# Prompt attention with every matrix product over 128 rows and 128 columns of TensorE

## The chip, the cores and the metric

One core of a Trainium2 chip runs the whole program. The metric is device time in microseconds. Five engines work beside each other, each in its own order: TensorE (PE; its weight loads are shown as PEld), VectorE (DVE), ScalarE (ACT), GpSimd (POOL) and SyncE (SP, which issues most transfers).

## What is computed

The program is one step of a decoder with two layers, for 1024 prompt tokens and 8 sampled tokens (each with 8192 past tokens in a paged cache). Each layer is

```
h = rms_norm(x) ; proj = h @ w_in                # inputs of four groups and a gate z
groups: NSA attention | HGRN2 recurrence | pooling | memory cross-attention
x = x + (silu(z) * concat(groups)) @ w_out
```

The change lies in two of the groups, and there in the prompt's tokens alone. NSA attention has 4 query heads of width 64 over one key-value head, and three branches whose results are gated and added:

```
s_c = q @ kcc.T ; p_c = masked_softmax(s_c)      # 32 compressed blocks of the prompt
s_s = q @ ks.T  ; p_s = masked_softmax(s_s)      # selected blocks (for this length: all causal keys)
s_w = q @ kw.T  ; p_w = masked_softmax(s_w)      # causal window of 512 keys
o = g0 * (p_c @ vcc) + g1 * (p_s @ vs) + g2 * (p_w @ vw)
```

Memory cross-attention has 4 heads of width 64 over 256 memory rows, without a mask. Everything is float32. TensorE multiplies in fp32r, in which an operand is split into a high part and a low rest (hi + lo), so that a product of two operands takes two or three passes.

## The kernel before

Each layer has four phases: A (norm and token-major projections), P2 (prompt attention, memory attention, pooling, and the rest of the projections as filler), P3 (compression of the sampled tokens' cache, recurrence, window) and O (output projection, selected branch of the sampled tokens). The change touches P2.

In P2, `nsa_prompt` goes through 8 tiles of 128 tokens. `nsa_prep` builds for a tile the queries `QS` (partitions 0 to 63 hold one half of hi and lo, 64 to 127 the other, so that one product over 128 rows gives (q_hi + q_lo) · k_hi with the keys' high part `KD` standing twice), the keys' low part `KL` (twice as well), the values `VS` as [hi | lo] in 128 columns, and the compressed branch's probabilities `Pc`, 32 columns a head. `nsa_unit` then works on two of the four heads: for each head and branch the scores' product (line 764), the causal mask as a product of a bf16 identity with a bf16 mask (lines 766 and 768), and the low keys' product, which takes only the 64 rows with the queries' high part (line 769):

```
mm(S, QS[half, h], KL[half, br, ks], start=False, stop=True)
```

VectorE takes the maximum (772), ScalarE the exponential (447), VectorE or GpSimd scales the probabilities (799, 797). They are then transposed in pieces of 128 keys, two pieces for both heads into one bank (`tr`, line 246), cast to hi on ScalarE (819), the rest lo on VectorE (820), and multiplied with the values: hi with 128 columns [hi | lo] (825, 828), lo with the 64 columns of the high values only (826). The compressed piece is the first of the list, with 32 rows, so its pair is cast in two parts. `fold` adds the two column halves of the result.

`mem_unit` does the same for the memory: lines 1150 and 1151 give the scores (the latter over 64 rows), 1168, 1170 and 1171 the values (1170 with 64 columns). The generator `others` runs its units and the pooling group between the units of `nsa_unit`.

The order of instructions on each engine is the planner's: it simulates a time line from its own costs and the priorities given with `prio`. The filler is `stageA2`, three products (lines 120 to 122) of 344 columns for each of 8 chunks, tied with `issue_after` to shares of the attention's own TensorE instructions, so that it is spread between them. PSUM banks of P2: two for scores, three for transposes, one accumulator, and two for the filler.

Of the kernel before, what the change touches and what calls it, by code (L numbers as in the profile page):

```python
# [9 lines left out]
F32 = mybir.dt.float32  # L10
# [80 lines left out]
class Lane:  # L91
    """PSUM tiles of one stream of work: s scores, t transposes, a accumulators, as (columns, buffers); own: tags with a pool for each bank"""
# [20 lines left out]
class Net:  # L113
# [14 lines left out]
    def cc(self, pool, name):  # L128
        """a constant that only one stage uses"""
# [22 lines left out]
    def rsqrt(self, y, x, pool, tag="rs"):  # L152
        """y = x ** -0.5 for [p, n] views"""
# [11 lines left out]
    # ---------------------------------------------------------------- setup  # L165
    def setup(self, ctx):
# [5 lines left out]
        self.identb = self.cp.tile([128, 128], BF, name="identb")  # L172
        self.mdiag = self.cp.tile([128, 128], BF, name="mdiagb")
        self.mfar = self.cp.tile([128, 128], BF, name="mfarb")
# [20 lines left out]
        self.zero = self.cp.tile([128, 320], F32, name="zero")  # L195
# [3 lines left out]
    def late_setup(self, tp):  # L199
        """constants that the first stage does without"""  # L200
        nc, a = self.nc, self.a
        nc.vector.tensor_copy(self.identb, self.ident)
# [5 lines left out]
        # numbers of the row pairs of every other four pages, among all row pairs of the cache  # L208
# [39 lines left out]
    # ---------------------------------------------------------------- stage A: norm and projections  # L248
# [23 lines left out]
    def alloc_hT(self, l, hp):  # L272
# [4 lines left out]
        nc.vector.tensor_copy(self.hS.rearrange("p k c -> p (k c)"), self.zero)  # L277
# [22 lines left out]
    def tokmajor(self, w, n, i, pieces, out, xp, lo_out=False):  # L300
        """out [p, n] = rows of token tile i times w; pieces: stationary views per k, sampled tokens as [hi | lo]"""
# [23 lines left out]
    def stageA1(self, l, wp, xp):  # L325
        """token-major projections: NSA queries, keys, values and gates, HGRN values, memory queries"""
# [34 lines left out]
    def stageA2(self, l, mts, wp, xp, **kw):  # L361
        """feature-major projections, one block of 128 features at a time"""
# [21 lines left out]
    def headnorm(self, x, gain, pool, tag):  # L384
        """x [p, h, 64] normalised over 64 in place; gain [p, 64] or [p, h, 64]"""
# [84 lines left out]
    def cpe(self, l, wp):  # L470
        """position rows with the halves of the feature axis as the weights have them"""
# [21 lines left out]
    def cweights(self, l, cp):  # L493
        """first layer's weights, a piece [128, 8, 256] for each half of the positions; w[t][c] = (hi, lo)"""
# [16 lines left out]
    def cload(self, l, u, g, xp, rb):  # L511
        """raw rows of 8 pages: two tokens to a partition; gives the pairs of [k0 k1] and of [v1 v0]; no u: the prompt's rows"""
# [62 lines left out]
    def csilu(self, hid, n, bB, xp):  # L575
        """2 silu of the hidden rows, feature-major, split"""
# [20 lines left out]
    def cout(self, hh, hl, n, W):  # L597
# [5 lines left out]
        # the values' two products with the weights' halves lie side by side  # L603
# [20 lines left out]
    def cprompt(self, l, wp, xp, other):  # L624
        """the 32 blocks of the prompt, in float32 products: the weights pass once"""
# [5 lines left out]
        for t in range(2):  # L631
# [20 lines left out]
            # what the position rows give alone is the bias of the sampled tokens' blocks  # L652
# [5 lines left out]
        # for the heads of either half: [hi | lo of that half's rows]  # L658
        nc.vector.tensor_copy(self.Kc.rearrange("p e s n -> p (e s n)"), self.zero[:, :128])
# [8 lines left out]
        nc.scalar.copy(self.VcP[:, 0:64], vc)  # L668
        nc.vector.tensor_tensor(self.VcP[:, 64:128], vc, self.VcP[:, 0:64].bitcast(F32), op=OP.subtract)

    # ---------------------------------------------------------------- stage B: mixing
    def oput(self, c, col, n, o):
        """spill a piece of the mixed features (feature-major) until the output projection"""
        self.nc.sync.dma_start(self.od[c][:, col:col + n], o)

    def nsa_prompt(self, l, pp, wk, other):
        """one step of the other stream after each pair of heads"""
# [3 lines left out]
        mcmp = self.cc(pp, "mcmp")  # L681
        nxt = self.nsa_prep(0, KV, mcmp, wk)
# [11 lines left out]
    def nsa_prep(self, i, KV, mcmp, wk):  # L694
        """queries [hi; lo] of token tile i, its keys and values, probabilities of the compressed branch"""
# [25 lines left out]
        # compressed branch  # L721
        Pc = wk.tile([128, 4, 32], F32, name="Pcmp")
# [13 lines left out]
        # rows without a complete block have no such branch  # L736
# [4 lines left out]
        return QS, Pc  # L741

    def nsa_unit(self, i, hp, QS, KV, Pc, wk, oT):
# [11 lines left out]
        for e in range(2):  # L755
            h = 2 * hp + e
            half = slice(e * 64, e * 64 + 64)
            for br in range(2):
                n = nw if br else nk
                c1 = n if C == 1 else (384 if br else 512)  # L760
                for c, (c0, m) in enumerate(((0, c1), (c1, n - c1))[:C]):
# [21 lines left out]
        else:  # L783
            # bring the chunks to their common maximum
# [10 lines left out]
        for p, w in chunks:  # L795
# [4 lines left out]
        jobs = [(None, 32, self.VcP)] + [(1024 + 128 * j, 128, VS[:, w0 // 128 + j, 1]) for j in range(nw // 128)] \  # L800
            + [(128 * j, 128, VS[:, j, 0]) for j in range(i + 1)]
        O = self.psA()
        last = len(jobs) - 1
        for g in range(0, len(jobs), 2):
            pair = jobs[g:g + 2]
            ps = self.psT()
            kmax = max(k for _, k, _ in pair)
            for j, (c0, k, _) in enumerate(pair):
                for e in range(2):
                    src = Pc[:, 2 * hp + e] if c0 is None else Pt[:, e, c0:c0 + k]  # L810
                    self.tr(ps[:k, j * 256 + e * 128:j * 256 + e * 128 + 128], src)
            ph = wk.tile([128, 512], F32R, name="ph", bufs=2)
            pl = wk.tile([128, 512], F32R, name="pl", bufs=2)
            if all(k == kmax for _, k, _ in pair):
                sp = [(kmax, 0, 256 * len(pair))]
            else:
                sp = [(k, 256 * j, 256 * j + 256) for j, (_, k, _) in enumerate(pair)]
# [987 lines left out]
```

## Time and profile before

| | |
|---|---|
| time, median of 3 runs | 2352.56 us (2349.35 to 2356.87) |
| span of the profiled execution | 2347.0 us |
| PE busy | 2133.6 us, 91% (14396 products) |
| PEld busy | 1831.8 us, 78% |
| DVE busy | 1535.0 us, 65% |
| ACT busy | 892.9 us, 38% |
| POOL busy | 751.9 us, 32% |

The time of the profiled execution itself is not listed; its span runs from its first to its last instruction, and the median of the timed runs lies 5.6 us above it. Busy times are sums over the span, and engines overlap. A product's duration in a row contains its way through the array, which overlaps the next product; the distance from one start to the next is what the stream of products pays.

### The profile page before, as it was taken

The numbers are of one execution on the slowest core, as the hardware profiler recorded it, in microseconds if no ns is written. First come the engines' busy times: TensorE is split into PE (matmuls) and PEld (weight loads), VectorE is DVE, ScalarE is ACT, GpSimd is POOL, SyncE is SP. The second block draws the span as 40 slices with busy tenths as digits, with TensorE's granted clock in tenths as the row PEclk, the third lists the DMA queues.
The fourth block names the chain that finished last, engine by engine and source line by source line (L and its number), as shares of the span: only waits on it lengthen the run. The fifth ranks groups of instructions, "written<-read, shape, count | busy, mean of one in ns | idle before, by whom it ended". The sixth has DMA issues, their size and how long they took to land.

```text
span 2347.0 us, 42103 instructions
## 1 busy us (share of the span) xinstructions
PE 2133.6 (91%) x14396; PEld 1831.8 (78%) x14396; DVE 1535.0 (65%) x4069; ACT 892.9 (38%) x2145; POOL 751.9 (32%) x837
## 2 busy tenths in 40 slices
PE   4999999999699999889969999999986899999898
PEld 4997887777588888777669978777776788887775
DVE  7874355797687776575288723678876777765643
ACT  4223355655443333331152234555546333322311
POOL 2002111422465554342220011233134556642430
PEclk8999997999699999989989999989987999999899
DMA  6236321211865455867453362211147455557672
GB/s 240 96 113 185 89 61 36 68 40 59 220 174 141 131 143 129 234 197 218 152 171 105 112 154 82 73 47 52 34 108 206 134 140 147 143 158 226 187 221 106
DMA packets 324094, 312.98 MB, mean 133 GB/s; under 512 B 60619, under 2 KB 285783, under 8 KB 323608
## 3 DMA queue, kind: packets, MB, share of 16 engines
q1 hardware_dynamic: 261544, 213.25, 31.2%
q0 software_dynamic: 24320, 79.71, 11.7%
q10 hardware_dynamic: 38016, 17.32, 2.8%
q8 instruction: 115, 1.88, 0.3%
q14 instruction: 99, 0.81, 0.1%
HBM read 255.00 MB, written 59.57 MB: 134 GB/s over the span
## 4 chain that ended last, share of the span: by engine, by line
PE 58%; DVE 13%; DMA 12%; issue 7%; POOL 5%; ACT 3%; SPq 1%; ACTq 0%; DVEq 0%; POOLq 0%
PE mt L246 4%; DMA R<-in_cache_nsa_dram 3%; PE aa L122 3%; PE aa L121 3%; DMA R<-in_cache_nsa_dram,idxc 3%; PE aa L120 3%; PE oa L122 2%; PE oa L120 2%; PE oa L121 2%; PE ch L122 2%; PE ch L120 2%; PE ms L769 2%; PE ch L121 2%; PE ct L246 2%; PE fa L120 2%
## 5 line engine op out<-in xcount | busy, mean ns | idle before, releaser
L524 POOL DMA_INDIRECT R<-in_cache_nsa_dram,idxc x256 | 253.0, 988 | 226.8 <-PE ct L246 138.6
L120 PE MATMUL ch<-w1h,Xh 128*128 128x256 f32 x1024 | 310.6, 303 | 10.3 <-ACT Xh L564 9.2
L122 PE MATMUL ch<-w1h,Xl 128*128 128x256 f32 x1024 | 309.4, 302 | 7.7 <-DVE Xl L565 7.5
L121 PE MATMUL ch<-w1l,Xh 128*128 128x256 f32 x1024 | 306.6, 299 | 0.0
L120 PEld LDWEIGHTS ch<-w1h,Xh 128*128 128x128 f32 x1024 | 207.3, 202 | 14.8 <-ACT Xh L564 10.9
L122 PEld LDWEIGHTS ch<-w1h,Xl 128*128 128x128 f32 x1024 | 207.4, 203 | 14.0 <-DVE Xl L565 10.5
L148 POOL TENSOR_TENSOR wl<-wf,wh 128x1024 fp32r<-128x1024 f32 (+2 forms) x42 | 92.7, 2217 | 374.7 <-ACT wh L139 293.6
L121 PEld LDWEIGHTS ch<-w1l,Xh 128*128 128x128 f32 x1024 | 207.3, 202 | 3.4 <-issue 2.1
L564 ACT CAST Xh<-ct 128x512 fp32r<-128x512 f32 x256 | 145.6, 585 | 146.5 <-PE ct L246 100.9
L246 PE MATMUL ct<-cst,R 128*128 128x128 f32 x1024 | 161.3, 287 | 37.6 <-DVE Xl L565 32.7
L565 DVE TENSOR_TENSOR Xl<-ct,Xh 128x512 fp32r<-128x512 f32 x256 | 171.1, 681 | 25.8 <-ACT Xh L564 25.0
L544 DVE COPY R<-R 128x256 f32<-128x256 f32 x260 | 95.1, 383 | 117.2 <-DMA R<-in_cache_nsa_dram,idxc 100.4
L120 PE MATMUL aa<-wh,hTh 128*128 128x326 f32 (+1 forms) x512 | 156.6, 307 | 5.2 <-ACT wh L139 5.2
L121 PE MATMUL aa<-wl,hTh 128*128 128x326 f32 (+1 forms) x512 | 156.4, 306 | 3.8 <-POOL wl L148 3.8
L246 PEld LDWEIGHTS ct<-cst,R 128*128 128x128 f32 x1024 | 118.5, 146 | 48.6 <-DVE Xl L565 33.3
L122 PE MATMUL aa<-wh,hTl 128*128 128x326 f32 (+1 forms) x512 | 155.9, 305 | 0.0
L772 DVE TENSOR_REDUCE nst<-ms 128x1 f32<-128x512 f32 (+3 forms) x192 | 99.0, 520 | 69.3 <-PE ms L769 66.8
L120 PE MATMUL fa<-hTh,wh 128*128 128x344 f32 x384 | 132.7, 346 | 2.5 <-ACT fo L381 2.5
L819 ACT CAST ph<-mt 128x512 fp32r<-128x512 f32 (+2 forms) x192 | 90.6, 484 | 100.9 <-PE ma L825 47.5
L447 ACT ACTIVATE P<-ms,nst 128x512 f32<-128x512 f32 (+3 forms) x192 | 106.1, 554 | 58.9 <-DVE nst L772 56.9
L121 PE MATMUL fa<-hTl,wh 128*128 128x344 f32 x384 | 128.0, 333 | 0.0
L122 PE MATMUL fa<-hTh,wl 128*128 128x344 f32 x384 | 127.9, 333 | 0.0
(559 smaller groups left out, 5763.8 us busy)
## 6 DMA issues: line engine op xcount, KB each, us to landing
wf<-in_w_in_dram SPq DMA_DIRECT2D x34, 512.0 KB
R<-in_cache_nsa_dram SPq DMA_DIRECT2D x256, 64.0 KB
R<-in_cache_nsa_dram ACTq DMA_DIRECT2D x256, 64.0 KB
zd<-fo SPq DMA_DIRECT2D x48, 172.0 KB
pwf<-in_cmp_w_dram SPq DMA_DIRECT2D x32, 256.0 KB
wof<-in_w_out_dram SPq DMA_DIRECT2D x16, 512.0 KB
oo<-od SPq DMA_DIRECT2D x16, 512.0 KB
oz<-zd SPq DMA_DIRECT2D x16, 512.0 KB
```

What stands on the lines that cost most here:

```text
L120: mm(out, lh, rh, start=first, stop=False)
L121: mm(out, lh, rl, start=False, stop=False)
L122: mm(out, ll, rh, start=False, stop=last)
L148: e.tensor_tensor(lo, src, hi.bitcast(F32), op=OP.subtract)
L246: self.nc.tensor.transpose(out, in_, self.ident[:in_.shape[0], :in_.shape[0]])
L447: self.nc.scalar.activation(out, S, AF.Exp, bias=nm, accum_out=sm)
L524: nc.gpsimd.indirect_dma_start(R[:, j].rearrange("p c d -> p (c d)"), None, rows, bass.IndirectOffsetOnAxis(ap=self.idxc[:, l, at + j:at + ...
L544: nc.vector.tensor_copy(Rs[:, :, :, 2], R[:, :, 0:2])
L564: nc.scalar.copy(hi, pv)
L565: nc.vector.tensor_tensor(lo, pv, hi.bitcast(F32), op=OP.subtract)
L772: nc.vector.tensor_reduce(one(nm), S, axis=AX.X, op=OP.max, negate=True)
L819: nc.scalar.copy(ph[:k, a0:a1], ps[:k, a0:a1])
```

## The change

The low keys are multiplied over all 128 rows in both attentions (the queries' low part times the keys' low part is added with them). The masks and their identity are kept in fp32r. The compressed values and probabilities are padded with zeros to 128, in two buffers that are cleared once a layer, and their piece is treated like the others. The low probabilities meet all 128 columns of the values. A constant of zeros shrinks to one column and is broadcast. Comments and docstrings go.

```diff
-        self.identb = self.cp.tile([128, 128], BF, name="identb")
-        self.mdiag = self.cp.tile([128, 128], BF, name="mdiagb")
-        self.mfar = self.cp.tile([128, 128], BF, name="mfarb")
+        self.identr = self.cp.tile([128, 128], F32R, name="identr")
+        self.mdiag = self.cp.tile([128, 128], F32R, name="mdiagr")
+        self.mfar = self.cp.tile([128, 128], F32R, name="mfarr")
...
-        self.zero = self.cp.tile([128, 320], F32, name="zero")
+        self.zero = self.cp.tile([128, 1], F32, name="zero")
...
+        nc.vector.tensor_copy(self.VcP, self.zero.to_broadcast([128, 128]))
+        nc.scalar.copy(self.VcP[:32, 0:64], vc)
...
+        self.Pcs = [pp.tile([128, 4, 128], F32, name=f"Pcmp{j}") for j in range(2)]
+        for x in self.Pcs:
+            nc.gpsimd.memset(x, 0.0)
...
-        Pc = wk.tile([128, 4, 32], F32, name="Pcmp")
+        Pf = self.Pcs[i % 2]
+        Pc = Pf[:, :, 0:32]
...
                     if c0 + m == n:
-                        mm(S[:, m - 128:m], self.identb, self.mdiag, start=False, stop=False)
+                        mm(S[:, m - 128:m], self.identr, self.mdiag, start=False, stop=False)
                     if br == 1 and i >= 4 and c == 0:
-                        mm(S[:, 0:128], self.identb, self.mfar, start=False, stop=False)
-                    mm(S, QS[half, h], KL[half, br, ks], start=False, stop=True)
+                        mm(S[:, 0:128], self.identr, self.mfar, start=False, stop=False)
+                    mm(S, QS[:, h], KL[:, br, ks], start=False, stop=True)
...
-            for (k, a0, a1) in sp:
-                nc.scalar.copy(ph[:k, a0:a1], ps[:k, a0:a1])
-                nc.vector.tensor_tensor(pl[:k, a0:a1], ps[:k, a0:a1], ph[:k, a0:a1].bitcast(F32), op=OP.subtract)
-            for j, (_, k, V) in enumerate(pair):
-                first, lst = g + j == 0, g + j == last
+            n = 256 * len(pair)
+            nc.scalar.copy(ph[:, :n], ps[:, :n])
+            nc.vector.tensor_tensor(pl[:, :n], ps[:, :n], ph[:, :n].bitcast(F32), op=OP.subtract)
+            for j, (_, V) in enumerate(pair):
                 cs = slice(j * 256, j * 256 + 256)
-                if not lst:
-                    mm(O[:, :256], V[:k, 0:128], ph[:k, cs], start=first, stop=False)
-                mm(O[:64, :256], V[:k, 0:64], pl[:k, cs], start=False, stop=False)
-                if lst:
-                    mm(O[:, :256], V[:k, 0:128], ph[:k, cs], start=False, stop=True)
+                mm(O[:, :256], V, ph[:, cs], start=g + j == 0, stop=False)
+                mm(O[:, :256], V, pl[:, cs], start=False, stop=g + j == last)
...
-            mm(sv[:, j], QM[half, h, tok], ML[half, h], start=False, stop=True)
+            mm(sv[:, j], QM[:, h, tok], ML[:, h], start=False, stop=True)
...
-        mm(O[:, :256], MV[:, 0, h], ph[:, 0:256], start=True, stop=False)
         for k in range(2):
-            mm(O[:64, :256], MV[:, k, h, 0:64], pl[:, k * 256:k * 256 + 256], start=False, stop=False)
-        mm(O[:, :256], MV[:, 1, h], ph[:, 256:512], start=False, stop=True)
+            for x in (ph, pl):
+                mm(O[:, :256], MV[:, k, h], x[:, k * 256:k * 256 + 256], start=k == 0 and x is ph, stop=k == 1 and x is pl)
```

## Rows read from the trace of the kernel before

**Rows 1.** Engines by stretch, P2 of layer one, both halves; columns as headed:

```profile
core 0: us, PE busy (x) PEld busy (x) DVE busy (x) ACT busy (x) POOL busy (x), PEclk, DMA share, GB/s
205.00:400.00 195.00, 187.79 (x1021) 155.26 (x1020) 88.47 (x243) 89.52 (x260) 38.25 (x32) 0.92 0.30 83
400.00:605.00 205.00, 188.66 (x1088) 149.00 (x1086) 163.04 (x397) 112.30 (x306) 63.81 (x58) 0.94 0.25 67
```

**Rows 2.** Chain of waits, shares by line, of 205 to 400 and 400 to 605 us:

```profile
by line: PE fa L120 10.3%; PE fa L121 9.8%; PE fa L122 9.3%; PE mt L246 9.0%; PE fx L120 6.4%; PE fx L121 5.9%; PE fx L122 5.7%; DMA pwf<-in_cmp_w_dram 5.2%; PE ms L1151 5.0%; PE ms L769 3.9%; PE ms L1150 3.7%; PE fx L646 3.4%; PE ms L764 2
...
by line: PE mt L246 12.7%; DVE P L799 10.1%; PE ms L769 8.8%; DMA R<-in_cache_nsa_dram 7.3%; PE ms L764 5.8%; PE ma L825 5.7%; PE ma L826 5.4%; issue 5.1%; PE fx L121 3.1%; DVE pl L820 2.7%; PE ma L1536 2.7%; PE fx L122 2.7%; PE fx L120 2.7
```

**Rows 3.** TensorE in order of time, output projection: start us, us, instruction:

```profile
1074.82 0.39 PE L120 MATMUL oa<-woh,oyh 128*128 128x512 f32 x1
1075.05 0.39 PE L121 MATMUL oa<-wol,oyh 128*128 128x512 f32 x1
```

**Rows 4.** TensorE in order of time near 480 us, rows*columns of the array before shapes:

```profile
480.39 0.38 PE L825 MATMUL ma<-ph,VcP 32*128 32x256 f32 x1
...
481.04 0.28 PE L826 MATMUL ma<-pl,VS 128*64 128x256 f32 x1
481.16 0.28 PE L825 MATMUL ma<-ph,VS 128*128 128x256 f32 x1
```

**Rows 5.** TensorE in order of time near 441 to 445 us:

```profile
441.65 0.40 PE L764 MATMUL ms<-KD,QS 128*128 128x512 f32 x1
441.98 0.49 PE L769 MATMUL ms<-KL,QS 64*128 64x512 f32 x1
442.40 0.39 PE L825 MATMUL ma<-ph,VS 128*128 128x256 f32 x1
442.63 0.32 PE L120 MATMUL fx<-hTh,wh 128*128 128x344 f32 x1
...
444.04 0.22 PE L764 MATMUL ms<-KD,QS 128*128 128x128 f32 x1
444.10 0.23 PE L766 MATMUL ms<-mdiagb,identb 128*128 128x128 bf16 x1
...
444.92 0.60 PE L246 MATMUL mt<-cst,qkvt 128*128 128x128 f32 x4
445.27 0.40 PE L120 MATMUL fx<-hTh,wh 128*128 128x344 f32 x1
```

**Rows 6.** TensorE in order of time near 295 us, a memory unit:

```profile
294.58 0.28 PE L1150 MATMUL ms<-MK,QMm 128*128 128x256 f32 x1
294.78 0.38 PE L1151 MATMUL ms<-ML,QMm 64*128 64x256 f32 x1
295.10 0.33 PE L764 MATMUL ms<-KD,QS 128*128 128x128 f32 x1
295.26 0.23 PE L766 MATMUL ms<-mdiagb,identb 128*128 128x128 bf16 x1
```

**Rows 7.** Line 769 by stretch, line 1151 early; then lines 825, 826 whole span:

```profile
205.00:400.00 195.00, 10.42 (x25) 4.87 (x25) 0.92 0.30 83
400.00:605.00 205.00, 31.00 (x71) 12.97 (x71) 0.94 0.25 67
...
205.00:400.00 195.00, 12.23 (x30) 5.89 (x30) 0.92 0.30 83
...
L825 PE MATMUL ma<-ph,VcP 32*128 32x256 f32 x32 | 12.6, 393 | 1.4 <-DVE poc L1538 1.1 <-DVE moT L1174 0.2
L826 PE MATMUL ma<-pl,VS 128*64 128x256 f32 x264 | 74.1, 307 | 8.6 <-DVE pl L820 8.4
```

**Rows 8.** VectorE by shape, line 820: count, busy us, mean ns, idle before:

```profile
L820 DVE TENSOR_TENSOR pl<-mt,ph 128x512 fp32r<-128x512 f32 x104 | 70.7, 683 | 14.1 <-ACT ph L819 12.2 <-PE ma L826 1.3
L820 DVE TENSOR_TENSOR pl<-mt,ph 128x256 fp32r<-128x256 f32 x56 | 23.2, 414 | 9.7 <-PE ma L826 5.5 <-ACT ph L819 4.0
L820 DVE TENSOR_TENSOR pl<-mt,ph 32x256 fp32r<-32x256 f32 x32 | 13.0, 407 | 8.5 <-ACT ph L819 8.3
```

**Rows 9.** Engines by stretch, around one dip of the granted clock (PEclk):

```profile
385.00:405.00 20.00, 19.27 (x61) 13.74 (x61) 8.94 (x23) 8.54 (x28) 3.12 (x3) 0.57 0.05 15
```

More of the change, by code (lines that the diff above doesn't have):

```diff
@@ L201, in late_setup @@
         nc, a = self.nc, self.a
-        nc.vector.tensor_copy(self.identb, self.ident)
+        nc.vector.tensor_copy(self.identr, self.ident)
         nc.vector.tensor_copy(self.mdiag, self.cc(tp, "mdiag"))
@@ L276, in alloc_hT @@
         self.hS = hp.tile([128, KT, 40], F32R, name="hS")
-        nc.vector.tensor_copy(self.hS.rearrange("p k c -> p (k c)"), self.zero)
+        nc.vector.tensor_copy(self.hS.rearrange("p k c -> p (k c)"), self.zero.to_broadcast([128, KT * 40]))
     def norm_tile(self, l, i, x, gB, xp):
@@ L657, in cprompt @@
         pk = self.cout(hh, hl, 32, (None, None, w2))
-        nc.vector.tensor_copy(self.Kc.rearrange("p e s n -> p (e s n)"), self.zero[:, :128])
+        nc.vector.tensor_copy(self.Kc.rearrange("p e s n -> p (e s n)"), self.zero.to_broadcast([128, 128]))
         for e in range(2):
@@ L667, in cprompt @@
         nc.vector.tensor_tensor(vc, pk[:32, 128:192], vc, op=OP.add)
-        nc.scalar.copy(self.VcP[:, 0:64], vc)
-        nc.vector.tensor_tensor(self.VcP[:, 64:128], vc, self.VcP[:, 0:64].bitcast(F32), op=OP.subtract)
+        nc.vector.tensor_copy(self.VcP, self.zero.to_broadcast([128, 128]))
+        nc.scalar.copy(self.VcP[:32, 0:64], vc)
+        nc.vector.tensor_tensor(self.VcP[:32, 64:128], vc, self.VcP[:32, 0:64].bitcast(F32), op=OP.subtract)
     def oput(self, c, col, n, o):
@@ L740, in nsa_prep @@
         nc.gpsimd.tensor_tensor(Pc, Pc, cm.unsqueeze(2).to_broadcast(bc), op=OP.mult)
-        return QS, Pc
+        return QS, Pf
     def nsa_unit(self, i, hp, QS, KV, Pc, wk, oT):
@@ L756, in nsa_unit @@
             h = 2 * hp + e
-            half = slice(e * 64, e * 64 + 64)
             for br in range(2):
@@ L799, in nsa_unit @@
                 nc.vector.tensor_scalar(p, p, w, None, op0=OP.mult)
-        jobs = [(None, 32, self.VcP)] + [(1024 + 128 * j, 128, VS[:, w0 // 128 + j, 1]) for j in range(nw // 128)] \
-            + [(128 * j, 128, VS[:, j, 0]) for j in range(i + 1)]
+        jobs = [(None, self.VcP)] + [(1024 + 128 * j, VS[:, w0 // 128 + j, 1]) for j in range(nw // 128)] \
+            + [(128 * j, VS[:, j, 0]) for j in range(i + 1)]
         O = self.psA()
@@ L806, in nsa_unit @@
             ps = self.psT()
-            kmax = max(k for _, k, _ in pair)
-            for j, (c0, k, _) in enumerate(pair):
+            for j, (c0, _) in enumerate(pair):
                 for e in range(2):
-                    src = Pc[:, 2 * hp + e] if c0 is None else Pt[:, e, c0:c0 + k]
-                    self.tr(ps[:k, j * 256 + e * 128:j * 256 + e * 128 + 128], src)
+                    src = Pc[:, 2 * hp + e] if c0 is None else Pt[:, e, c0:c0 + 128]
+                    self.tr(ps[:, j * 256 + e * 128:j * 256 + e * 128 + 128], src)
             ph = wk.tile([128, 512], F32R, name="ph", bufs=2)
             pl = wk.tile([128, 512], F32R, name="pl", bufs=2)
[L814 to L817, printed above, removed]
-            for (k, a0, a1) in sp:
-                nc.scalar.copy(ph[:k, a0:a1], ps[:k, a0:a1])
-                nc.vector.tensor_tensor(pl[:k, a0:a1], ps[:k, a0:a1], ph[:k, a0:a1].bitcast(F32), op=OP.subtract)
-            for j, (_, k, V) in enumerate(pair):
-                first, lst = g + j == 0, g + j == last
-                cs = slice(j * 256, j * 256 + 256)
-                if not lst:
-                    mm(O[:, :256], V[:k, 0:128], ph[:k, cs], start=first, stop=False)
-                mm(O[:64, :256], V[:k, 0:64], pl[:k, cs], start=False, stop=False)
-                if lst:
-                    mm(O[:, :256], V[:k, 0:128], ph[:k, cs], start=False, stop=True)
+            n = 256 * len(pair)
+            nc.scalar.copy(ph[:, :n], ps[:, :n])
+            nc.vector.tensor_tensor(pl[:, :n], ps[:, :n], ph[:, :n].bitcast(F32), op=OP.subtract)
+            for j, (_, V) in enumerate(pair):
+                cs = slice(j * 256, j * 256 + 256)
+                mm(O[:, :256], V, ph[:, cs], start=g + j == 0, stop=False)
+                mm(O[:, :256], V, pl[:, cs], start=False, stop=g + j == last)
         self.fold(O[:, :256], oT, 0, wk)
@@ L1588, in osamp @@
         y = self.sy = xp.tile([128, KT, 40], F32R, name="sy", bufs=1)
-        nc.vector.tensor_copy(y.rearrange("p k c -> p (k c)"), self.zero)
+        nc.vector.tensor_copy(y.rearrange("p k c -> p (k c)"), self.zero.to_broadcast([128, KT * 40]))
         nc.vector.tensor_tensor(o[:, 2:], o[:, 2:], z[:, 2:], op=OP.mult)
@@ L1636, in layer_params @@
         self.Kc = lp.tile([128, 2, 2, 32], F32R, name="Kc")
-        self.VcP = lp.tile([32, 128], F32R, name="VcP")
+        self.VcP = lp.tile([128, 128], F32R, name="VcP")
         self.cbias = lp.tile([128, 2, 256], F32, name="cbias")
```

## The prediction

> **What bounds the kernel now.** I read the stretches by engine first, then the chain of waits in them, then the order of instructions on TensorE. Only the two stretches of prompt attention matter, one per layer, since nearly every edit with a price lies there: 205 to 605 us in the first layer and its twin in the second. The reader is to see that TensorE is busy 187.8 of 195 us in the early half and 188.7 of 205 us in the late half, while VectorE goes from 88.5 to 163.0 us [rows 1]. So TensorE bounds the early half outright; the late half is shared, with VectorE at 80%. The chain of waits says the same: early, it is almost wholly TensorE, with lines 1151, 769 and 1150 holding 5.0, 3.9 and 3.7%; late, line 769 alone holds 8.8% and line 764 5.8%, but VectorE's scaling of the probabilities (line 799) holds 10.1% [rows 2].
>
> Busy time hides what matters here, so I read starts. Full-array products follow one another by their columns: 512 columns 0.23 us [rows 3], 256 columns 0.12 us (481.04 to 481.16) [rows 4], 128 columns 0.06 us (444.04 to 444.10) [rows 5]. Products over 64 rows do not. At 441.65 a full product of 512 columns takes 0.33 us until the 64-row one starts, that one 0.42 us until the next starts, and the next, full again with 256 columns, 0.23 us [rows 5]. The time is lost on both sides of the odd product: about 0.10 before, 0.19 after, and 0.11 at the following product.
>
> **The change part by part.**
>
> *Low halves over all rows (lines 769 and 1151).* Price of one: 442.63 − 441.65 = 0.98 us, against 0.23 + 0.23 + 0.12 = 0.58 if all three were full, so 0.40 [rows 3 to 5]. In the memory branch: 294.58 to 295.26 is 0.68 us, against 0.12 + 0.12 + 0.06 = 0.30, so 0.38 [rows 4 to 6]. I take 0.39. In the first layer 25 + 71 products of line 769 and 30 of line 1151 early, the other 2 late [rows 7]: 55 early, 73 late, or 21.5 and 28.5 us. The products over full rows multiply more terms but stream the same columns.
>
> The Trainium skill says the same of rows, and more: by "TensorEngine Tiling (Array Packing)", section Key Properties, changing the tiling mode drains TensorE. If a 64-column product counted as such a change, it would drain too; the trace says it doesn't, since line 826 (64 columns) and line 825 (128) start 0.12 us apart [rows 4].
>
> *Compressed values and probabilities padded to 128.* Two products over 32 rows per pair of heads go: 480.39 to 481.04 is 0.65 us, against 3 × 0.12 = 0.36, so 0.29, plus the entry that here coincides with the exit of line 769 [rows 4]. I take 0.35 (bounds 0.29 and 0.40); 32 such pairs [rows 7], 16 a layer, 5 of them early: 1.8 and 3.9 us. Padding also lets the first two pieces share one cast and one subtraction: on VectorE 407 + 414 ns become 683 ns, 0.14 us less, 16 times a layer = 2.2 us [rows 8]; ScalarE's cast merges likewise. VectorE holds a part of the late chain only, so I count 0.5 us. Two memsets on GpSimd are new in each layer, at the head of a stretch in which it is busy 38 of 195 us [rows 1]: nothing, and if uncovered the first tile's probabilities wait for them once a layer, about a microsecond.
>
> *Masks and identity in fp32r.* The bf16 weight load becomes one of 4 bytes an element. No row has such a mask product between full ones. Below, it is the 0.06 us of 128 columns, nothing lost; above, the four 128-column fp32 transposes that start 0.35 us before the next product, 0.09 each [rows 5]. I take the upper end, being nearest in shape: 0.03 us for each of the 128 diagonal masks and of the 32 far ones (the latter at windows of tiles 4 to 7), 80 a layer = 2.4 us.
>
> *Low probabilities against 128 columns of values.* A weight load of 128 columns instead of 64, under a 256-column product. The 128-column loads of line 825 keep the 0.12 us rhythm in the same rows [rows 4], so nothing; without that cover 0.05 us each, for the 264 of line 826 on values [rows 7] and as many of the memory branch as of line 1151, some 16 us in all.
>
> The order of products within a pair, the zero that shrinks to one column and the retyped constants add no work on these engines in this stretch.
>
> *How much is on the path.* Early, line 1151 holds 5.0% of 195 = 9.8 us of the chain, as much as its 30 products take from start to start at 0.32 [rows 2, 6, 7]; line 769 7.6 us. Practically all is on the path; I take 0.8, as near-equal chains (weights of the compressed branch, transposes) come up. Late, line 769 holds 8.8% of 205 = 18 us; 71 products at 0.31 to 0.42 would be 26, so 0.7 is on the path. VectorE's scaling is next in line there: I take 0.55. Sum for a layer: 0.8 × (21.5 + 1.8) + 0.55 × (28.5 + 3.9) = 18.6 + 17.8 = 36.4; masks −2.4 × 0.6 = −1.4; VectorE +0.5; together 35.5.
>
> *Clock.* From 385 to 405 us TensorE ran at a granted 0.57, thus largely at 1.2 GHz, with only 61 products in 20 us [rows 9]. The early half has 0.92 and the late 0.94 [rows 1], so up to 15.6 + 12.3 = 28 us a layer of clock is missing. Denser products may lift it, longer waits for VectorE may lower it. I count 3.5 us a layer, less than half of the 0.43 × 20 = 8.6 us of that one dip.
>
> Total: 2 × 39 = 78 us. The profiled span is 2347.0 us; the median of the runs, 2352.56, lies 5.6 us above it, which I take for what lies around the span. 2347.0 − 78 + 5.6 = 2274.6, so **2275 us**.
>
> **The rivals.**
>
> *All of it lands on the path.* TensorE is the order-setting engine throughout, VectorE and ScalarE wait for scores less, and the clock's dips go. 55.7 − 2.4 = 53.3 us a layer plus half the missing clock, 14: 135 us, **2218**; without the clock 2246. For it: TensorE's busy share in both halves. Against: the 0.7 above and line 799 in the chain.
>
> *VectorE becomes the bound late.* It has 163 us of work in 205 [rows 1]. If its idle 42 us can only shrink to some 35, the late half gives 7 us: 18.6 + 7 − 1.4 = 24 a layer, **2304**.
>
> *The clock falls (slower).* TensorE finishes early, waits for VectorE in the late half, and runs it at 1.2 GHz. Late work of TensorE would be 188.7 − 32 = 156 us at full clock; each microsecond of wall time at half clock costs up to half a microsecond. The point from which it decides: 39 us a layer, some 78 us more at half clock in that half. At 110 us the loss is 55, net 16 a layer, **2385**. For it: dips stand behind waits already. Against: 0.94 with VectorE at 80%.
>
> *Nothing changes.* The gaps around line 769 belong to something else, such as the score bank being accumulated again. Then 0 to −5 us: **2350**. Against: line 120's products accumulate in one bank at full pace [rows 3]. A rule of the Trainium skill would also give it: in "TensorE: Matmul & The Clock Gate", section LDWEIGHTS (loading the stationary operand), a load takes the time of its columns, however few the rows, so that full rows save nothing by themselves. The trace agrees on a lone product and not on the neighbours.
>
> *The 64-column products drain too.* Then 264 + 64 more products give 0.39 each, 128 us, two thirds of it on the path: **2190**. The 0.12 us rhythm of line 826 speaks against it [rows 4].
>
> **How the numbers follow.** Forecast 62 in 100, its own range 2252 to 2296; all on the path 13; VectorE bound 16; clock 4; nothing 4; columns 1. The range 2235 to 2312 takes in most of the first three and leaves out the rest, under 2 in 10. 0.3% is 7 us, about what runs of this kernel can tell apart. Faster: 62 + 13 + 16 + 1 = 92; within 0.3%: 4; slower: 4.
>
> **What the profile after would show.** Right: lines 769 and 1151 as 128*128, starting 0.23, 0.17 or 0.12 us ahead of what follows; the two stretches some 36 to 40 us shorter each, the others unmoved; no 32-row products; mask products 0.09 us or less apart. VectorE's share late should rise to about 88%, and TensorE should wait for line 799 longer than now. Wrong: the same gaps around full-row products (then rows were not the cause), stretches shortened only early (VectorE), a granted clock under 0.85 in the late half, or products of line 826 more than 0.13 us apart.

## The result, and the profile after

The changed kernel takes 2277.72 us (median of 4 runs, 2273.36 to 2284.6), the kernel before 2350.95 us in the same comparison (2349.09 to 2356.87): a ratio of 0.9694, 95% interval 0.9648 to 0.974. Forecast were 2275 us, within 2235 to 2312. The profiled execution took 2284.6 us, the slowest of the four, with a span of 2282.8 us, 64.2 us less than the span of before. In one later round of runs (masks in bf16, no scaling, 384 columns, early entry) the kernel before took 2405 us, so those four are judged by their ratios to it.

I measure an attention stretch from the first product with the weights `pwf` (the prompt's compressed blocks) to the end of the last fold. It went from 403.4 to 364.6 us in the first layer and from 399.1 to 364.4 in the second: −38.8 and −34.7, where 36 to 40 were forecast. The sum, 73.5, is more than the span lost: 9.3 us came back elsewhere. The first fence shows the stretches by engine, each cut where its work comes late (the counterpart of [rows 1]), and below them the 25 us behind the end of the first.

```profile
core 0: us, PE busy (x) PEld busy (x) DVE busy (x) ACT busy (x) POOL busy (x), PEclk, DMA share, GB/s
206.00:385.00 179.00, 167.72 (x1084) 151.59 (x1084) 97.39 (x252) 94.34 (x269) 40.67 (x35) 0.98 0.33 90
385.00:571.00 186.00, 158.56 (x1020) 142.22 (x1018) 152.47 (x374) 105.07 (x280) 64.17 (x57) 0.93 0.28 76
1330.00:1515.00 185.00, 172.79 (x1120) 156.53 (x1119) 102.43 (x264) 101.18 (x287) 47.76 (x40) 0.98 0.33 91
1515.00:1694.00 179.00, 151.20 (x980) 136.97 (x978) 148.43 (x360) 98.38 (x263) 56.82 (x52) 0.93 0.28 74
571.00:596.00 25.00, 7.06 (x30) 5.11 (x30) 16.92 (x25) 13.62 (x18) 12.70 (x10) 0.50 0.76 205
```

TensorE is still busy 94% of the early stretch, but only 85% of the late one; VectorE stands there at 82 and 83%. In the 25 us behind the last fold TensorE has 7 us of work.

The next fence is TensorE in order of time after the change, three places: a memory unit, a pair with the compressed values (`VcP`), and scores with masks. Columns as in [rows 4]; lines 1146, 1147, 769, 771, 773, 774, 823 and 824 were 1150, 1151, 764, 766, 768, 769, 825 and 826 of before.

```profile
227.35 0.28 PE L1146 MATMUL ms<-MK,QMm 128*128 128x256 f32 x1
227.47 0.28 PE L1147 MATMUL ms<-ML,QMm 128*128 128x256 f32 x1
227.59 0.28 PE L1146 MATMUL ms<-MK,QMm 128*128 128x256 f32 x1
...
409.23 0.36 PE L823 MATMUL ma<-ph,VcP 128*128 128x256 f32 x1
409.43 0.28 PE L824 MATMUL ma<-pl,VcP 128*128 128x256 f32 x1
409.55 0.28 PE L823 MATMUL ma<-ph,VS 128*128 128x256 f32 x1
...
444.38 0.42 PE L769 MATMUL ms<-KD,QS 128*128 128x384 f32 x1
444.64 0.22 PE L773 MATMUL ms<-mfarr,identr 128*128 128x128 f32 x1
444.70 0.39 PE L774 MATMUL ms<-KL,QS 128*128 128x384 f32 x1
444.93 0.60 PE L246 MATMUL mt<-cst,P 128*128 128x128 f32 x4
```

The memory pair of [rows 6] took 0.32 us for its low product; here each product starts 0.12 behind the last. The mask is 0.06 long. The low product behind it takes 0.23 for 384 columns, which would be 0.17 by its columns: 0.05 is left, and the experiment with bf16 masks bears on it.

The waits of TensorE in the late part, before (400 to 605 us) and after (385 to 571); columns: who waited, for whom, us in total, times, longest.

```profile
PE mt L246 <- DVE P L799: 7.3, 4, 3.9
PE ma L826 <- DVE pl L820: 2.8, 3, 2.3
```

```profile
PE mt L246 <- DVE P L804: 9.2, 10, 4.4
PE ma L824 <- DVE pl L820: 7.2, 8, 1.8
PE ms L769 <- ACT P L447: 3.3, 6, 0.9
PE ma L823 <- ACT ph L819: 2.7, 1, 2.7
```

TensorE is early now and waits for VectorE's and ScalarE's pieces: 16.4 us for VectorE's two lines against 10.1. Over a whole stretch its idle time rose by 13.8 and 14.7 us (24.8 to 38.6, 24.2 to 38.9). The chain of waits late in the second layer now begins with VectorE at 11.1%, and the low product (line 774) is down to 3.2%; before, in the same layer from 1560 to 1770 us, transposes led with 12.4%, then VectorE's scaling with 9.3% and the low product (line 769) with 9.2%. In the first layer the chain after the change does not pass through the stretch.

```profile
by line: DVE P L804 11.1%; PE mt L246 7.2%; DMA stXh<-in_cmp_w_dram 7.1%; issue 7.0%; DMA R<-in_cache_nsa_dram,idxc 5.7%; DVE nst L777 4.6%; DVE pl L820 4.0%; PE ma L823 3.3%; PE ma L824 3.3%; PE ms L774 3.2%; PE ms L769 3.0%; PE fx L120 2.
```

VectorE's subtraction by shape (against [rows 8]) shows the merged first pair: 32 pieces over 32 rows are gone, and as many of 256 columns have become pieces of 512.

```profile
L820 DVE TENSOR_TENSOR pl<-mt,ph 128x512 fp32r<-128x512 f32 x136 | 92.2, 684 | 22.1 <-ACT ph L819 19.4 <-PE ma L823 1.4 <-PE mt L246 0.5
L820 DVE TENSOR_TENSOR pl<-mt,ph 128x256 fp32r<-128x256 f32 x24 | 10.0, 416 | 6.9 <-ACT ph L819 6.7
```

### The profile page after: what moved, and what is told of

Its sections match the earlier page's. It is cut to its first block, busy times and chain, and to the rows that moved or that the text cites. A ratio compares the mean times of both kernels' runs of the same rounds, so it can differ in the third digit from the quotient of the medians.

```text
span 2282.8 us, 42061 instructions
## 1 busy us (share of the span) xinstructions
PE 2032.7 (89%) x14396; PEld 1811.7 (79%) x14396; DVE 1532.5 (67%) x4039; ACT 881.5 (39%) x2109; POOL 744.2 (33%) x841
## 4 chain that ended last, share of the span: by engine, by line
PE 25%; DVE 10%; DMA 8%; issue 5%; POOL 3%; SPq 2%; ACT 1%; ACTq 0%; DVEq 0%; POOLq 0%
DMA R<-in_cache_nsa_dram,idxc 2%; POOL R L524 2%; PE mt L246 1%; PE aa L121 1%; PE aa L122 1%; PE aa L120 1%; DMA oo<-od 1%; PE oa L121 1%; PE oa L120 1%; PE oa L122 1%; DVE P L804 1%; PE ch L120 1%; PE fa L120 1%; PE ch L122 1%; PE mt L1428 1%
## 5 line engine op out<-in xcount | busy, mean ns | idle before, releaser
L120 PE MATMUL ch<-w1h,Xh 128*128 128x256 f32 x1024 | 310.7, 303 | 13.8 <-ACT Xh L564 12.7
L122 PEld LDWEIGHTS ch<-w1h,Xl 128*128 128x128 f32 x1024 | 204.7, 200 | 13.1 <-DVE Xl L565 9.0
L820 DVE TENSOR_TENSOR pl<-mt,ph 128x512 fp32r<-128x512 f32 (+1 forms) x160 | 101.1, 644 | 28.9 <-ACT ph L819 26.0
```

Source lines behind the costliest of these rows:

```text
L120: mm(out, lh, rh, start=first, stop=False)
L122: mm(out, ll, rh, start=False, stop=last)
L820: nc.vector.tensor_tensor(pl[:, :n], ps[:, :n], ph[:, :n].bitcast(F32), op=OP.subtract)
```

## The experiments

Ratios are to the kernel before, run beside each; the changed kernel's own ratio came out at 0.9694 and, repeated, at 0.9749, so smaller differences between experiments mean little. "Stretch" is the attention stretch as above, first and second layer, in the one profiled execution of each run; the changed kernel's two profiles differ by 3.2 and 1.6 us. "Switches" counts neighbours on TensorE whose rows change between 128, 64 and 32 or fewer: 842 before, 258 after. Code is shown in cuts, marked with dots.

**Low halves alone over full rows**, on the kernel before:

```diff
-                    mm(S, QS[half, h], KL[half, br, ks], start=False, stop=True)
+                    mm(S, QS[:, h], KL[:, br, ks], start=False, stop=True)
...
-            mm(sv[:, j], QM[half, h, tok], ML[half, h], start=False, stop=True)
+            mm(sv[:, j], QM[:, h, tok], ML[:, h], start=False, stop=True)
```

> The kernel before with one edit: the low keys' products of lines 769 and 1151 take all 128 rows. Theory (each 64-row product between full ones costs 0.39 us of TensorE's order, 256 of them, two thirds to four fifths on the path): most of the whole change, about -62 us, 2284 to 2295; the two attention stretches each some 33 us shorter; start-to-start of line 769 falls from 0.31-0.42 us to 0.12-0.23 us. Rival (the gain comes from fewer instructions and merged casts of the padded piece): under -15 us, 2336 or more.

Measured: 2291.6 against 2348.32 us, ratio 0.9734 (0.967 to 0.9798); stretches 366.8 and 372.4 us, −36.6 and −26.7; switches 352. Two edited lines bring a gain that the noise does not tell from that of the whole change. The time lies in the range expected; the second layer's stretch gained less than the 33 us expected. In order of time the low product is now followed after 0.20 us behind a mask and after 0.23 for 512 columns:

```profile
431.04 0.28 PE L764 MATMUL ms<-KD,QS 128*128 128x256 f32 x1
431.16 0.23 PE L766 MATMUL ms<-mdiagb,identb 128*128 128x128 bf16 x1
431.20 0.36 PE L769 MATMUL ms<-KL,QS 128*128 128x256 f32 x1
431.40 0.32 PE L122 MATMUL fa<-hTh,wl 128*128 128x344 f32 x1
...
432.48 0.40 PE L769 MATMUL ms<-KL,QS 128*128 128x512 f32 x1
432.71 0.28 PE L826 MATMUL ma<-pl,VS 128*64 128x256 f32 x1
```

**Padding alone**, on the kernel before (compressed values and probabilities over 128 rows, first pair cast at once):

```diff
...
-        jobs = [(None, 32, self.VcP)] + [(1024 + 128 * j, 128, VS[:, w0 // 128 + j, 1]) for j in range(nw // 128)] \
+        jobs = [(None, 128, self.VcP)] + [(1024 + 128 * j, 128, VS[:, w0 // 128 + j, 1]) for j in range(nw // 128)] \
...
-        self.VcP = lp.tile([32, 128], F32R, name="VcP")
+        self.VcP = lp.tile([128, 128], F32R, name="VcP")
```

> The kernel before with one edit: compressed values and probabilities padded with zeros to 128 rows, their cast and subtraction merged with the next piece's. Theory (32 pairs of 32-row products at 0.35 us, two thirds on the path, plus a little of the merged VectorE work): -6 to -12 us, 2339 to 2345. Rival (the merge of the casts relieves VectorE, which binds the late half): over -20 us.

Measured: 1.003 (0.9996 to 1.0064), stretches 401.7 and 399.6 us: no gain, a miss. TensorE's work did fall, but its waits grew as much (the table below). And the first product of the compression stage (`ch`), which began 1.2 us before the last fold, begins 20.9 and 24.2 us behind it, as in the changed kernel.

**The change without padding** (all its other edits):

> The changed kernel with the padding undone alone: compressed values and probabilities in 32 rows, cast by themselves; full rows for the low keys, fp32r masks and 128 columns for the low probabilities stay. Theory (padding saves 16 passages of 32-row pairs a layer at 0.35 us, two thirds on the path, and loses 8 us a layer at the entry of the compression stage): the attention stretches 3 to 5 us longer each than those of the changed kernel, the first products at the last fold, in all 0.994 to 1.000 of the changed kernel, and slower than the version with moved buffers by 6 to 10 us. Rival (the padding is worth nothing even where the entry is undisturbed): equal to the version with moved buffers within 0.2%.

Measured: 0.9758 (0.9731 to 0.9784), 2292.75 us; stretches 380.6 and 374.3 us, 16.0 and 9.9 longer than in the changed kernel (19.2 and 11.5 longer than in its repetition below). Expected were 3 to 5 us. But the low halves alone, without padding as well, had 366.8 and 372.4 us, only 2.2 and 8.0 longer than the changed kernel, and masks and columns, which are the other difference, cost nothing in the two runs that follow. So the 10 to 19 us can't be put down to padding; part of it is the clock (44.4 and 37.5 us at 1.2 GHz here, 32.1 and 32.0 in the changed kernel). The changed kernel, run beside it, took 2286.67 us: the 6 us between them are within the noise, and what padding is worth in the total is not shown.

**The changed kernel with low probabilities against 64 columns again**:

```diff
...
-                mm(O[:, :256], V, pl[:, cs], start=False, stop=g + j == last)
...
+                mm(O[:64, :256], V[:, 0:64], pl[:, cs], start=False, stop=False)
...
```

The memory attention is edited in the same way.

> The changed kernel with one part undone: the low probabilities meet 64 columns of values again (lines 824 and 1166), rows stay at 128. Theory (a change of columns alone costs nothing, the weight load is hidden): within 8 us of the changed kernel, 2270 to 2286, spacing of these products 0.12 us as before. Rival (columns drain the array as rows do): 328 products at 0.39 us, two thirds on the path, some +80 us, about 2360.

Measured: 0.9713 (0.9676 to 0.9749), stretches 362.2 and 362.3 us: nothing given up. In its order of time (rows*columns before the shapes) 64 and 128 columns follow each other at the same 0.11 to 0.12 us:

```profile
485.23 0.28 PE L825 MATMUL ma<-ph,VS 128*128 128x256 f32 x1
485.34 0.28 PE L826 MATMUL ma<-pl,VS 128*64 128x256 f32 x1
485.46 0.28 PE L825 MATMUL ma<-ph,VS 128*128 128x256 f32 x1
```

By the Trainium skill, "TensorEngine Tiling (Array Packing)", section Key Properties, a change of tiling mode drains TensorE. The runs agree for rows, at the prices below, and show no drain from a change of columns.

**The changed kernel with masks in bf16**:

```diff
...
-                        mm(S[:, m - 128:m], self.identr, self.mdiag, start=False, stop=False)
+                        mm(S[:, m - 128:m], self.identb, self.mdiag, start=False, stop=False)
...
```

> The changed kernel with one part undone: masks and identity in bf16 again. Theory (mask products cost 0.06 us either way, or up to 0.03 us more in fp32r): within 6 us of the changed kernel, 2270 to 2284. Rival (changing between bf16 and fp32r costs a passage of its own, as rows do): 160 mask products at 0.2 us or more, +20 us.

Measured: 0.9738 (0.9679 to 0.9798), 2345.99 against 2405.04 us; stretches 366.9 and 369.5 us: no passage of its own, as expected. In order of time:

```profile
448.61 0.28 PE L769 MATMUL ms<-KD,QS 128*128 128x256 f32 x1
448.74 0.23 PE L771 MATMUL ms<-mdiagb,identb 128*128 128x128 bf16 x1
448.77 0.36 PE L774 MATMUL ms<-KL,QS 128*128 128x256 f32 x1
448.98 0.32 PE L121 MATMUL fx<-hTl,wh 128*128 128x344 f32 x1
```

Starts by the medians at full clock: main product 0.123, mask 0.039, low product 0.203, together 0.365 us; with fp32r masks 0.119 + 0.060 + 0.172 = 0.351. The mask itself is shorter in bf16; what follows it pays more back. The low product's weight load takes 0.201 us behind a bf16 mask and 0.188 behind one in fp32r; that this is the reason is not shown. Over a whole stretch TensorE's work is the same with either mask (the table below).

**One 64-row product written as two**, on the kernel before, each over half the columns:

```diff
-                    mm(S, QS[half, h], KL[half, br, ks], start=False, stop=True)
+                    k0 = w0 * br + c0
+                    for p in range(2):
+                        mm(S[:, p * m // 2:(p + 1) * m // 2], QS[half, h], KL[half, br, k0 + p * m // 2:k0 + (p + 1) * m // 2], start=False, stop=p == 1)
```

> The kernel before with each 64-row score product of line 769 written as two products of half the columns, both over 64 rows, one right behind the other in nearly all of the 192 cases (96 in each layer). Theory (what costs is the passage from 128 rows to 64 and back, paid once in either kernel): the second half starts behind the first at the pace of its columns, about 0.06 to 0.12 us, and the attention stretches stay within 6 us of the kernel before; ratio to the kernel before 1.000 to 1.006. Rival (a 64-row product is slow by itself, wherever it stands): each second half adds about 0.3 to 0.39 us of its own, two thirds of it on the path, so the two stretches are 15 to 25 us longer each and the ratio is 1.012 to 1.022.

Measured: 2365.48 against 2345.09 us, 1.011 (1.005 to 1.017); stretches 418.3 and 421.0 us. The total lies between the two expectations and the stretches, 15 and 22 us longer, in the rival's range, so I go by the starts (x2 is the pair):

```profile
560.14 0.47 PE L764 MATMUL ms<-KD,QS 128*128 128x512 f32 x1
560.55 0.50 PE L771 MATMUL ms<-KL,QS 64*128 64x256 f32 x2
560.98 0.49 PE L764 MATMUL ms<-KD,QS 128*128 128x512 f32 x1
...
565.31 0.23 PE L768 MATMUL ms<-mfarb,identb 128*128 128x128 bf16 x1
565.47 0.46 PE L771 MATMUL ms<-KL,QS 64*128 64x192 f32 x2
565.86 0.39 PE L827 MATMUL ma<-ph,VS 128*128 128x256 f32 x1
```

Two halves of 256 columns take 0.43 us from their start to the next product, the whole 512 columns 0.42 [rows 5]; for 384, 256 and 128 columns the medians rise from 0.368 to 0.394, 0.311 to 0.365 and 0.254 to 0.337. So an added 64-row product costs 0.006 to 0.083 us, not the 0.3 to 0.39 of the rival: 96 a layer are 28 × (0.006 + 0.026 + 0.054) + 12 × 0.083 = 3.4 us. The passage is what costs. The theory's detail was off: the second half starts 0.105 us later than its columns, and the exit behind the pair is shorter for it. TensorE's work in the stretches agrees: it grew by 2.8 and 1.0 us (the table below). The rest of the 15 and 22 us is time lost at 1.2 GHz, 7.0 and 19.3 us more (TensorE spent 68.7 and 85.9 us of the stretches at that clock, against 54.6 and 46.0), and waits, 5.0 and 1.5 more. Why the clock fell more often there is not shown.

**Score products of two chunks interleaved**, on the kernel before, so that two 64-row products would be neighbours:

> The kernel before with the scores of two chunks interleaved: both full products and masks first, then both 64-row products one behind the other. As many 64-row products as before, half as many passages from 128 to 64 rows and back (96 fewer). Theory (the passage costs, not the 64 rows): 37 us less in TensorE's order, part of it lost because both score banks must be free at once: -10 to -30 us, 2321 to 2341; second 64-row product of a pair starts 0.12 to 0.23 us after the first. Rival (a 64-row product is slow by itself, or accumulating twice in one bank is): no gain or slower, and the second 64-row product starts 0.31 to 0.42 us after the first.

Measured: 1.005 (1.0024 to 1.0075), but the planner put other products between them; 824 of 842 switches stayed. The gain that was expected did not come, and the run tells nothing of the question, which the run above answered.

**The changed kernel without VectorE's scaling** of chunks under 512 columns (line 804; those probabilities stay unscaled):

```diff
-            else:
-                nc.vector.tensor_scalar(p, p, w, None, op0=OP.mult)
```

> The changed kernel without VectorE's scaling of the probability chunks below 512 columns (line 804); this part of the computation is left out. Theory (after the change VectorE shares the bound of the late half): that half gives up a large part of the 39 us of scaling that lie on VectorE in each layer, -20 to -50 us in all, 2228 to 2258. Rival (TensorE alone still binds): under -8 us.

Measured: 0.9668 (0.9602 to 0.9734), stretches 355.5 and 359.7 us. VectorE loses 32 and 31 us of work a stretch (durations added up: 275.7 to 243.6, 277.1 to 246.4), the stretch only 9.1 and 4.7 against the first profile of the changed kernel, and 11.4 and 9.8 against the run with bf16 masks, made beside it. The theory that VectorE binds the late part, with 20 to 50 us, fell. By engine and by waits:

```profile
385.00:561.00 176.00, 150.87 (x998) 137.97 (x997) 132.32 (x324) 102.89 (x276) 60.12 (x55) 0.92 0.28 78
```

```profile
PE ma L821 <- ACT ph L817: 7.8, 2, 4.0
PE ma L822 <- DVE pl L818: 6.9, 4, 3.7
```

VectorE is down to 75%, and TensorE still waits 34.4 and 35.4 us in a stretch (38.6 and 38.9 in the changed kernel), now most for the casts of the transposed pieces. I read this as no single engine, but the dependence of scores, probabilities, transposes and casts on each other; no run tests that reading.

**The changed kernel with chunks of 384 columns scaled on GpSimd too**:

```diff
-            if p.shape[1] == 512:
+            if p.shape[1] >= 384:
```

> The changed kernel with the scaling of the 384-column chunks moved from VectorE to GpSimd. Theory (VectorE shares the bound of the late half, GpSimd has room there): 28 chunks a layer of 0.6 to 0.8 us leave VectorE, -8 to -20 us, 2258 to 2270. Rival (the two engines hinder each other, or TensorE waits for GpSimd's slower scaling at the end of a unit): no gain or slower.

Measured: 0.9754 (0.9698 to 0.981), stretches 360.9 and 363.7 us: no gain, though 8 to 20 us were expected.

**What the stretches consist of.** "Waits" are the idle times ahead of TensorE's products. "Clock" is what the rest lost at the granted clock of 1.2 GHz, each microsecond there counted half. "Work" is what is left: TensorE's products at full clock, with their gaps. First and second layer, in us:

| | work | clock | waits |
|---|---|---|---|
| before | 354.4, 354.9 | 24.2, 20.1 | 24.8, 24.2 |
| changed | 312.7, 312.1 | 13.3, 13.4 | 38.6, 38.9 |
| low halves alone | 320.2, 318.5 | 11.3, 16.4 | 35.3, 37.4 |
| padding alone | 346.5, 349.5 | 23.2, 20.3 | 32.0, 29.8 |
| changed without padding | 325.4, 324.3 | 17.5, 16.1 | 37.7, 33.8 |
| changed, 64 columns | 312.3, 312.5 | 8.4, 8.9 | 41.5, 41.0 |
| changed, masks in bf16 | 312.7, 312.0 | 13.1, 14.7 | 41.2, 42.9 |
| before, products split | 357.2, 355.9 | 31.2, 39.4 | 29.8, 25.7 |

About 1.4 us of the work saved with padding is no saving: with the late entry described next, 12 transposes (`ct`) a stretch have moved behind its end.

**What came back behind the stretch.** From the last fold to the last product of the compression stage the kernel before needs 421.1 and 427.2 us, the changed one 432.5 and 435.3. In the changed kernel, around the fold at 571.2 (TensorE in order of time, idle time before in brackets):

```profile
569.83 1.05 PE L246 MATMUL ct<-cst,R 128*128 128x128 f32 x4
575.97 0.48 PE L246 MATMUL mt<-cst,qs 8*128 8x8 f32 x4 [5.08 <-DMA qs<-qkvd]
579.87 2.10 PE L246 MATMUL ct<-cst,R 128*128 128x128 f32 x8 [3.42 <-DVE Xl L565]
584.81 1.11 PE L246 MATMUL ct<-cst,R 128*128 128x128 f32 x4 [2.84 <-DVE Xl L565]
590.37 1.11 PE L246 MATMUL ct<-cst,R 128*128 128x128 f32 x4 [4.45 <-DVE Xl L565]
```

Transposes and casts of the cache's rows (`ct`, `Xl`) run alone there; the first `ch` product starts 24.4 us behind the fold, 24 of these transposes stood ahead of the fold in the kernel before and 12 here. Three runs asked whether this late entry is the loss. One puts the two padded buffers into a pool of their own on the other side of memory:

```diff
...
-        self.Pcs = [pp.tile([128, 4, 128], F32, name=f"Pcmp{j}") for j in range(2)]
...
+                    pcp = pool(st, "pcp")
+                    self.Pcs = [pcp.tile([128, 4, 128], F32, name=f"Pcmp{j}") for j in range(2)]
...
```

> The changed kernel with the two padded probability buffers in a pool of their own on the other side of the memory, cleared at the same place of the program; the arithmetic is the same. Theory (the padded buffers shifted the attention's tiles in memory, so that the compression stage's first X tiles lie where late tiles of the attention live, and its first products come 24 us behind the last fold instead of 1 us ahead of it): the first products come at the last fold again, the stretch from the last fold to the last product of that stage shrinks by some 8 us a layer to 421 to 428 us, in all 0.993 to 0.996 of the changed kernel (-9 to -16 us). Rival (the entry is bound by its transfers and conversions, whichever products come first): within 0.2% of the changed kernel.

Measured: 0.9733 (0.9706 to 0.9761), 2285.02 us. The first `ch` product is 1.2 us ahead of the fold again, with 24 transposes before the fold, so the place of the buffers decides when the stage may enter. But the stage ends 417.2 and 437.7 us behind the fold, a gain in one layer and none in the other, and the total equals that of the changed kernel beside it:

> The changed kernel itself, as the measure for the two others on the same chip: ratio to the kernel before 0.965 to 0.974; first products of the compression stage some 24 us behind the last fold of the attention in both layers.

Measured: 2286.67 against 2345.27 us, 0.9749 (0.9725 to 0.9773), just above the range expected; stretches 361.4 and 362.8; 436.2 and 425.8 us from fold to the stage's end. With `moved`'s buffers the 25 us behind the fold look like this:

```profile
573.00:598.00 25.00, 11.81 (x69) 9.88 (x67) 16.39 (x27) 16.06 (x20) 15.78 (x13) 0.64 0.90 240
```

TensorE has 12 us of work in place of 7, transfers fill 90% of the time, and from 560 to 620 us its transposes wait 13.3 us for `Xl`, as in the changed kernel (13.2). The third run calls the compression stage's first steps earlier in the planner's order:

```diff
+                    self.lane = c
+                    self.prio(-0.5)
+                    gen = self.stageC(l, cp, 4)
+                    next(gen)
...
```

> The changed kernel with the entry of the compression stage (first rows, weights, first transposes) ahead of the recurrence's gates in the planner's order. Theory (the 8 to 11 us that the change gives back lie in the order at this entry, where VectorE and GpSimd work on gates while the first products wait for weights): -6 to -16 us, 2262 to 2272. Rival (the entry is bound by its transfers, near 200 GB/s): within 5 us of the changed kernel.

Measured: 0.9683 (0.9627 to 0.974); `ch` still begins 20.7 and 19.8 us behind the fold, and the stage ends 437.5 and 440.5 us behind it. It did not restore the entry, and so tells nothing of its worth. From the fold to the layer's last output product the kernels with the early entry (before, low halves alone, without padding, `moved`, split, interleaved) take 560 to 584 us, 570 on average, and those with the late one (changed, its repetition, 64 columns, padding alone) 570 to 585, 578 on average. That hints at some 8 us a layer, but the ranges overlap, and the one pair made for the question, `moved` and the changed kernel beside it, has equal totals. What gives the few microseconds back stays open; that the late entry does is not shown.

None of these kernels is clearly faster than the changed one.

## Why the prediction was right

*The price of 64 rows: right.* Medians over the 64-row products of the kernel before at full clock, each with full products around it and counted above 0.4545 ns a column, the pace of full products behind one another in these traces: line 769 costs 0.102 us ahead, 0.194 itself and 0.106 at the next, 0.402 in all (150 products); line 1151 0.178 + 0.195 + 0.111 = 0.488 (54). I had 0.39 for both, 0.10, 0.19 and 0.11 for its parts. After, 0.060 and 0.006 remain. But the second median counts twice: line 1150 often stands between two 64-row products, and its one distance then holds the exit of the first and the entry of the next. With line 1150 behind a product of the filler and no second pair following, line 1151 costs 0.093 + 0.195 + 0.108 = 0.396 (8 cases). So 0.39 was right for both. By these prices the saving is 0.34 × 96 + 0.39 × 32 = 45 us a layer, 50.0 forecast, since the low product behind a mask keeps 0.05. With the low halves alone, TensorE's work fell by 34.2 and 36.4 us, less than the prices add up to; where the other 9 to 11 us went is not shown. The added 64-row neighbours of the split run cost 0.08 at most.

*32-row pairs: a term near the mark, on a wrong picture, and no gain from it alone.* 5.7 us a layer were forecast. Padding alone took 7.9 and 5.4 us off TensorE's work; but the waits grew by 7.2 and 5.6, and the stretches gained 1.7 and −0.5. I had priced pairs, and only 15 of the 32 are neighbours: in the other 17 the filler, transposes or scores stand between the two products. Apart and between full products of the filler, the first costs 0.394 us (6 cases) and the second 0.343 (3). I had added edits; what a saving is worth depends on what else TensorE waits for.

*Masks: a small term that is nothing.* Forecast 0.03 us dearer each, measured 0.014 cheaper for the group of three at 256 columns, which would be +1.1 us a layer (80 × 0.014) for −1.4; TensorE's work over the stretch shows neither. I had looked at the mask alone, and its 0.06 us is what I had as the lower bound.

*64 columns: right.* No drain, and 128 columns in their place cost nothing; that rival is out.

*How much is on the path: the sum right, its parts not.* Forecast for a layer were 53.3 us of products, 17.8 of them lost to the path (53.3 − 35.5), and 3.5 of clock: 39.0. By the table TensorE's work fell by 41.7 and 42.8 us, the waits took 13.8 and 14.7 of it, and the clock gave 10.9 and 6.7: 38.8 and 34.8. So the products were sized 11 us too large and the clock 3 to 7 too small, and the loss to waits 3 to 4 too large. The early part's granted clock rose in the first layer from 0.92 [rows 1] to 0.98, the late one's fell from 0.94 to 0.93. The errors lie against each other, and that the total came out this close is partly luck: 78 us of gain were forecast, 73.2 were measured, but 64.2 between the two profiled spans and 58.6 when the comparison was repeated.

*VectorE late: right in direction, wrong in kind.* Waits for line 804 (799 of before) grew, but VectorE stands at 82 and 83%, not 88, and giving it 32 us less to do shortens the stretch by 5 to 11. The rival in which it becomes the bound is out: both halves of the gain are there.

*The surroundings: wrong.* I had them unmoved; 73.5 us of gain in the stretches became 64.2 in the span. I took the padded buffers for two memsets and did not ask what else wants their place in memory: they moved the entry of the next stage by some 25 us. Whether that is the loss could not be told.

*Around the span: wrong, without weight.* The profiled execution of after lies 1.8 us above its span. I had taken 5.6, the distance of a span from a median of other executions, which mixes the two.

*The other rivals.* The clock did not fall (0.943 over the span, 0.940 before). "Nothing changes" is out by the low halves alone. "All on the path", 2218, is out by the longer waits.

## What to carry to other kernels

Price an odd-shaped product by the starts of three instructions, the one ahead, itself and the next, not by its own duration; and where rows change from one product to the next, multiplying by zeros over full rows can be cheaper than leaving rows out. Of the time freed on TensorE about seven tenths came through here, beside a VectorE at 80%; the rest turned into waits. A new buffer can put off when the next stage gets its memory, even where its own instructions are free; whether that cost time here is not shown.

## What the hardware showed that I had not expected

The passages add up where they meet: line 1150 pays 0.094 us ahead of a 64-row product when a product of the filler stands before it (19 cases), and 0.198, an exit and an entry, when another line 1151 does (24 cases). A run of 64-row products pays the passage once: in the kernel before, eight 64-row products of the recurrence, 128 columns each, take 0.66 us together to the start of the next, where eight odd ones would lose 0.402 each:

```profile
662.92 0.72 PE L1433 MATMUL mt<-hKQ 64*128 64x128 f32 x8
663.58 0.66 PE L246 MATMUL ct<-cst,R 128*128 128x128 f32 x4
```

And a shorter product can cost more: the bf16 mask saved 0.021 us itself and the low product behind it took 0.031 longer.
